# The carry copies moved out of the Exp pair in a prefix log-sum-exp scan on one core

## Chip, cores, metric

One core of one Trainium2 chip. The metric is the device time of one execution in microseconds. Executions fall into states. "Slow" means over 1.5% above the fastest execution of the same kernel; means and ratios below use fast executions only.

## The reference

```python
B, S, D = (8, 4096, 2048)                      # float32
out[:, 0, :] = x[:, 0, :]
for t in range(1, S):                          # running log-sum-exp along S
    mx = np.maximum(out[:, t-1, :], x[:, t, :])
    out[:, t, :] = mx + np.log(np.exp(out[:, t-1, :] - mx) + np.exp(x[:, t, :] - mx))
```

The kernel computes it as log(cumulative sum(exp(x))). It works on 64 tiles of 128 partitions x 4 rows x 2048 columns (4 MB each): load, Exp, sums of four rows and across partitions, Ln, store.

## The kernel before

Six tile buffers `ti` stand in a ring. SyncE issues the loads, each when the store of the same buffer has landed. ScalarE does the Exp, a small copy and the Ln, in two halves of the columns, and issues the stores. The copy carries the last 32 partitions of the finished tile n-1 into `rs`, from which the sums of tile n are begun. It waits for DVE's last addition of tile n-1 (`joined`), and DVE's third addition of tile n waits for it (`copied`).

```python
            @block.sync
            def _(sp):
                ...
                        take(sp, stored[n], 16)                       # the buffer's store has landed
                        load(x_v[bass.ds(j * NI + n, 1)][0], n)
            @block.scalar
            def _(act):
                def exp(n, h, rows=slice(0, R)):
                    ...  # for h == 0: waits for the load; Exp in place; exps[h] += 1
                def copy(n, h, turn):
                    act.activation(
                        rs[P - 32:, half(h)], ti[n % NI][P - 32:, R - 1, half(h)], ACT.Copy
                    )._wait_ge(joined[h], turn + 1).then_inc(moved, 1)
                    event(act, [(moved, 2 * turn + h + 1)], [(copied[h], "sem-add-imm", 1)])
                ...
                with act.Fori(0, turns) as j:
                    for n in range(1, NI + 1):
                        for h in range(2):
                            exp(n, h)
                            copy(n - 1, h, n - 1)
                        for h in range(2):
                            ln(n - 1, h)
                        store(n - 1, o_v[bass.ds(j * NI + (n - 1), 1)][0], 2 * n)
                    settle(NI, NI, 2 * NI)
                ...
            @block.vector
            def _(dve):
                def local(n, h):
                    ...  # two additions, the first after exps[h]
                    dve.wait_ge(copied[h], n + 1)
                    dve.tensor_add(
                        rs[:P - 1, cols], t[:P - 1, 2, cols], t[:P - 1, 3, cols]
                    )._wait_ge(chain[h], 3 * n + 2).then_inc(sums[h], 1)
```

The softmax here doesn't subtract the row's maximum and nothing guards it: scores larger than these inputs give would overflow.

Of the kernel before, what the change touches and what calls it, by code (L numbers as in the profile page):

```python
# [9 lines left out]
def kernel(  # L10
# [30 lines left out]
    NT = B * NBLK  # L41
# [16 lines left out]
    def half(h):  # L58
        return slice(h * HALF, (h + 1) * HALF)

    def event(engine, waits, updates):

        engine.add_instruction(mybir.InstEventSemaphore(  # L63
            name=f"I-{nc.next_id()}", engine=engine.engine, ins=[], outs=[],
            sync_info=mybir.SyncInfo(
                on_wait=[mybir.SyncWait(
                    sync_type="semaphore", id=s.num, ant_name=s.name,
                    wait_mode="sem-ge-imm", wait_value=n,
                ) for s, n in waits],
                on_update=[mybir.SyncUpdate(  # L70
                    sync_type="semaphore", id=s.num, ant_name=s.name,
                    update_mode=mode, update_value=n,
                ) for s, mode, n in updates],
            ),
        ))

    def take(engine, s, n):

        event(engine, [(s, n)], [(s, "sem-sub-imm", n)])

    with tc.tile_critical():  # L81
# [12 lines left out]
        with nc.Block() as block:  # L94

            @block.gpsimd
            def _(g):
                g.memset(before[:], 1.0).then_inc(ones, 1)  # L98
                g.wait_ge(ones, 1)

                g.affine_select(  # L101
                    out=before[:], in_=before[:], compare_op=mybir.AluOpType.is_ge, fill=0.0,
                    base=-1, pattern=[[1, P]], channel_multiplier=-1,
                ).then_inc(shaped, 1)
                g.wait_ge(shaped, 1)

                g.affine_select(  # L107
                    out=before[:], in_=before[:], compare_op=mybir.AluOpType.is_ge, fill=1.0,
                    base=P - 2, pattern=[[0, P]], channel_multiplier=-1,
                ).then_inc(shaped, 1)  # L110

                for h in range(2):
                    g.sem_inc(copied[h], 1)
# [22 lines left out]
# [3 lines that stand above are left out]
                    t = ti[n % NI]  # L139
                    if h == 0:  # L140
                        take(act, loaded[n % NI], 16)
                    act.activation(  # L142
                        t[:, rows, half(h)], t[:, rows, half(h)], ACT.Exp
                    ).then_inc(exps[h], 1)
# [8 lines that stand above are left out]
                def ln(n, h, rows=slice(0, R)):  # L153
                    t = ti[n % NI]
                    act.activation(  # L155
                        t[:, rows, half(h)], t[:, rows, half(h)], ACT.Ln
                    ).then_inc(logs, 1)

                def store(n, dst, done, rows=slice(0, R)):
                    act.wait_ge(logs, done)  # L160
                    act.dma_start(  # L161
                        out=dst[:, rows, :], in_=ti[n % NI][:, rows, :]
                    ).then_inc(stored[n % NI], 16)

                def settle(turns, copies, done):
                    take(act, moved, 2 * copies)
                    take(act, joined[0], turns)
                    take(act, joined[1], turns)
                    take(act, logs, done)

                take(act, top, 16)
                act.activation(ti[0][:, 0:2, :], ti[0][:, 0:2, :], ACT.Exp)  # L172
                exp(0, 0, slice(2, R))
                exp(0, 1, slice(2, R))
                turns = (NT - 2) // NI
                with act.Fori(0, turns) as j:
                    for n in range(1, NI + 1):
                        for h in range(2):
                            exp(n, h)
                            copy(n - 1, h, n - 1)  # L180
                        for h in range(2):
                            ln(n - 1, h)
                        store(n - 1, o_v[bass.ds(j * NI + (n - 1), 1)][0], 2 * n)
                    settle(NI, NI, 2 * NI)
                first = turns * NI
                for n in range(first + 1, NT):

                    early = n == NT - 1
                    for h in range(2):
                        if not early:  # L190
                            exp(n, h)
                        copy(n - 1, h, n - 1 - first)
                        if early and h == 0:
                            ln(n - 1, h)
                        if early:
                            exp(n, h)
                    for h in range(early, 2):
                        ln(n - 1, h)
                    store(n - 1, o_v[n - 1], 2 * (n - first))

                turn = NT - 1 - first
                act.wait_ge(joined[0], turn + 1)
                ln(NT - 1, 0)
                act.wait_ge(joined[1], turn + 1)
                done = 2 * turn + 1
                for rows in LAST:
                    ln(NT - 1, 1, rows)
                    done += 1
                    store(NT - 1, o_v[NT - 1], done, rows)
                settle(NT - first, NT - 1 - first, done)  # L210
# [91 lines left out]
```

## Time and profile before

| | the kernel before |
|---|---|
| three timed executions | 1252.88, 1254.04, 1254.31 us |
| profiled execution | 1279.36 us, slow |
| DMA queues, share of 16 engines | loads 49.6%, stores 49.1% |
| busy: ScalarE, DVE, TensorE | 82%, 82%, 32% |
| load, store: issue to landing (median) | 36.8 us, 45.4 us |

The prediction shows how the profile of before is read. From the timeline of the kernel before (start, us, engine, line, operation; in brackets the idle time before it and what ended that):

```profile
23.14 3.62 ACT L142 ACTIVATE ti<-ti 128x4096 f32<-128x4096 f32 x1 [6.00 <-ACTq L63]
...
27.38 1.05 ACT L148 ACTIVATE rs<-ti 32x1024 f32<-32x1024 f32 x1 [0.62 <-DVE ti L253]
...
40.67 0.40 ACTq L161 DMA_DIRECT2D out_dram<-ti  x1
```

Exp of tile 1 runs as soon as its load is there, and the first store of the run is issued at 40.67 us.

### The profile page before, as it was taken

The numbers are of one execution on the slowest core, as the hardware profiler recorded it, in microseconds if no ns is written. First come the engines' busy times: TensorE is split into PE (matmuls) and PEld (weight loads), VectorE is DVE, ScalarE is ACT, GpSimd is POOL, SyncE is SP. The second block draws the span as 40 slices with busy tenths as digits, with TensorE's granted clock in tenths as the row PEclk, the third lists the DMA queues.
The fourth block names the chain that finished last, engine by engine and source line by source line (L and its number), as shares of the span: only waits on it lengthen the run. The fifth ranks groups of instructions, "written<-read, shape, count | busy, mean of one in ns | idle before, by whom it ended". The sixth has DMA issues, their size and how long they took to land. (4 is left out here: it accounts for less than half of the span.)

```text
span 1277.6 us, 3085 instructions
## 1 busy us (share of the span) xinstructions
PE 409.4 (32%) x512; PEld 131.9 (10%) x512; DVE 1044.3 (82%) x640; ACT 1053.0 (82%) x385; POOL 1.0 (0%) x7
## 2 busy tenths in 40 slices
PE   1334342324223242232422324233242341432412
PEld 0111110101001010010100101011010010110100
DVE  5999998878788787887878788787887888878874
ACT  5999998877878778787887878788788787888883
POOL 0000000000000000000000000000000000000000
PEclk9766567655666656766567666566666666656665
DMA  9999999999999999999999999999999999999976
GB/s 398 423 431 432 428 433 429 428 432 428 431 427 429 426 432 428 425 427 425 426 423 427 431 425 422 433 429 426 429 428 420 428 425 426 422 426 429 424 323 282
DMA packets 18727, 536.96 MB, mean 420 GB/s; under 512 B 2081, under 2 KB 2081, under 8 KB 2081
## 3 DMA queue, kind: packets, MB, share of 16 engines
q1 hardware_dynamic: 9360, 268.44, 49.6%
q10 hardware_dynamic: 9360, 268.44, 49.1%
q8 instruction: 4, 0.07, 0.0%
q14 instruction: 3, 0.02, 0.0%
HBM read 268.44 MB, written 268.44 MB: 420 GB/s over the span
## 5 line engine op out<-in xcount | busy, mean ns | idle before, releaser
L218 PE MATMUL ps<-rs,before 128*128 128x512 f32 (+1 forms) x512 | 409.4, 946 | 845.3 <-DVE rs L243 845.2
L142 ACT ACTIVATE ti<-ti 128x4096 f32<-128x4096 f32 (+1 forms) x128 | 459.4, 3590 | 186.1 <-ACTq L63 178.3
L155 ACT ACTIVATE ti<-ti 128x4096 f32<-128x4096 f32 x129 | 456.3, 3582 | 13.9 <-DVE ti L253 5.7
L249 DVE TENSOR_TENSOR ti<-ti,ps 128x3072 f32<-128x3072 f32 x128 | 428.4, 3347 | 1.1 <-PE ps L218 1.1
L236 DVE TENSOR_TENSOR ti<-ti 128x1024 f32<-128x1024 f32 x128 | 156.8, 1225 | 201.4 <-ACT ti L142 201.4
L218 PEld LDWEIGHTS ps<-rs,before 128*128 128x128 f32 (+1 forms) x512 | 131.9, 285 | 1121.4 <-DVE rs L243 1009.8
L253 DVE TENSOR_TENSOR ti<-ti 128x1024 f32<-128x1024 f32 x128 | 156.8, 1225 | 4.4
L243 DVE TENSOR_TENSOR rs<-ti 127x1024 f32<-127x1024 f32 x128 | 156.8, 1225 | 4.4
L239 DVE TENSOR_TENSOR ti<-ti 128x1024 f32<-128x1024 f32 x128 | 156.8, 1225 | 4.4
L148 ACT ACTIVATE rs<-ti 32x1024 f32<-32x1024 f32 x126 | 132.6, 1052 | 4.1 <-DVE ti L253 0.6
L172 ACT ACTIVATE ti<-ti 128x4096 f32<-128x4096 f32 x1 | 3.6, 3616 | 6.5 <-ACTq L63 6.5
L35 ACT ACT_TABLE_LOAD x1 | 1.3, 1283 | 0.8 <-PEq L286 0.8
L107 POOL TENSOR_SCALAR_AFFINE_SELECT before<-before 128x128 f32<-128x128 f32 x1 | 0.3, 292 | 0.1
L101 POOL TENSOR_SCALAR_AFFINE_SELECT before<-before 128x128 f32<-128x128 f32 x1 | 0.3, 292 | 0.1
L98 POOL MEMSET before<- 128x128 f32 x1 | 0.2, 204 | 0.5 <-SPq L81 0.5
L286 POOL MEMSET const-bfloat16-1.0<- 128x1 bf16 x1 | 0.1, 101 | 0.0
L286 POOL MEMSET const-uint8-127<- 128x1 uint8 x1 | 0.1, 101 | 0.0
L286 POOL MEMSET const-float32-0.0<- 128x1 f32 x1 | 0.1, 98 | 0.3 <-issue 0.3
L286 POOL MEMSET const-float32-1.0<- 128x1 f32 x1 | 0.1, 98 | 0.0
## 6 DMA issues: line engine op xcount, KB each, us to landing
ti<-in_x_dram SPq DMA_DIRECT2D x63, 4096.0 KB, 36.8
out_dram<-ti ACTq DMA_DIRECT2D x63, 4096.0 KB, 45.4
ti<-in_x_dram SPq DMA_DIRECT2D x2, 2048.0 KB, 9.6
out_dram<-ti ACTq DMA_DIRECT2D x2, 2048.0 KB, 10.6
```

Of the source, the lines that this page charges most:

```text
L35: nc.scalar.preload_act_table_set("natural_log_exp_and_others")
L142: act.activation(t[:, rows, half(h)], t[:, rows, half(h)], ACT.Exp).then_inc(exps[h], 1)
L148: act.activation(rs[P - 32:, half(h)], ti[n % NI][P - 32:, R - 1, half(h)], ACT.Copy)._wait_ge(joined[h], turn + 1).then_inc(moved, 1)
L155: act.activation(t[:, rows, half(h)], t[:, rows, half(h)], ACT.Ln).then_inc(logs, 1)
L172: act.activation(ti[0][:, 0:2, :], ti[0][:, 0:2, :], ACT.Exp)
L218: m = pe.matmul(ps[n % 2][:, sl], before[:k, :], rs[:k, sl], start=True, stop=True,)
L236: dve.tensor_add(t[:, 1, cols], t[:, 0, cols], t[:, 1, cols])._wait_ge(exps[h], n + 1).then_inc(chain[h], 1)
L239: dve.tensor_add(t[:, 2, cols], t[:, 1, cols], t[:, 2, cols])._wait_ge(chain[h], 3 * n + 1).then_inc(chain[h], 1)
L243: dve.tensor_add(rs[:P - 1, cols], t[:P - 1, 2, cols], t[:P - 1, 3, cols])._wait_ge(chain[h], 3 * n + 2).then_inc(sums[h], 1)
L249: dve.tensor_add(t[:, 0:3, cols], t[:, 0:3, cols], ps[n % 2][:, cols].unsqueeze(1).to_broadcast([P, 3, HALF]),)._wait_ge(ahead[h], n + 1). ...
L253: dve.tensor_add(t[:, 3, cols], t[:, 2, cols], t[:, 3, cols])._wait_ge(chain[h], 3 * n + 3).then_inc(joined[h], 1)
L286: nc = _bacc.Bacc("TRN2", target_bir_lowering=False, num_devices=1)
```

## The change

It is meant to fill ScalarE's wait for the load with the first copy, and to put the second one behind both Exp halves, so that the Exp pair runs without a gap.

```diff
+                def step(n, turn, early=False):
+                    copy(n - 1, 0, turn)
+                    if early:
+                        ln(n - 1, 0)
+                    exp(n, 0)
+                    exp(n, 1)
+                    copy(n - 1, 1, turn)
+                    if not early:
+                        ln(n - 1, 0)
+                    ln(n - 1, 1)
@@ in the loop
-                        for h in range(2):
-                            exp(n, h)
-                            copy(n - 1, h, n - 1)
-                        for h in range(2):
-                            ln(n - 1, h)
+                        step(n, n - 1)
@@ in the last steps (early: n is the last tile)
-                    (Exp, copy, Exp, copy, Ln, Ln; for the last tile copy, Ln, Exp, copy, Exp, Ln)
+                    step(n, n - 1 - first, n == NT - 1)
```

(The line in parentheses stands for eleven lines of the same kind, which are cut here.)

More of the change, by code (lines that the diff above doesn't have):

```diff
@@ L186, in _ @@
                 for n in range(first + 1, NT):
-                    early = n == NT - 1
-                    for h in range(2):
-                        if not early:
-                            exp(n, h)
-                        copy(n - 1, h, n - 1 - first)
-                        if early and h == 0:
-                            ln(n - 1, h)
-                        if early:
-                            exp(n, h)
-                    for h in range(early, 2):
-                        ln(n - 1, h)
+                    step(n, n - 1 - first, n == NT - 1)
                     store(n - 1, o_v[n - 1], 2 * (n - first))
```

## The prediction

> **What bounds the kernel now.** I read the page first, then the wait table, then stretches of time, one tile period of the timeline, and last the DMA record of the final 48 us. The profiled execution took 1279.36 us and is marked slow, against 1254.04 us for the timed runs. I take its order of events and its instruction times over to the fast runs, but not its length.
>
> From the page's DMA queues (packets, MB, share of 16 engines' span) and from the wait table (us in total, times, longest us):
>
> ```profile
> q1 hardware_dynamic: 9360, 268.44, 49.6%
> q10 hardware_dynamic: 9360, 268.44, 49.1%
> DVE ti L236 <- ACT ti L142: 201.4, 113, 15.4
> ACT ti L142 <- ACTq L63: 178.3, 63, 6.0
> ```
>
> The queue of the loads and the queue of the stores together hold the 16 DMA engines for 98.7% of the span. ScalarE waits 178.3 us in 63 waits ahead of an Exp, about 2.8 us a tile, for the load. That looks like time to be won, but the stretches say what stands behind it (columns: stretch and length, busy us of each engine, clock, DMA share, GB/s):
>
> ```profile
> 100.00:400.00 300.00, 103.54 (x128) 33.29 (x128) 258.77 (x159) 257.48 (x95) 0.00 (x0) 0.63 1.00 430
> 400.00:800.00 400.00, 128.45 (x160) 40.99 (x160) 324.74 (x200) 328.70 (x120) 0.00 (x0) 0.63 1.00 426
> 800.00:1180.00 380.00, 121.88 (x152) 39.11 (x152) 312.83 (x192) 315.04 (x115) 0.00 (x0) 0.64 1.00 427
> ```
>
> The DMA share is 1.00 throughout, while DVE (324.74 of 400) and ScalarE (328.70 of 400) are at 81 and 82%. A load is issued 36.8 us before it lands (median on the page) and a tile period is 20 us (400 us for 160/8 = 20 tiles), so the next load is always already queued when one lands. ScalarE waits for DMA bandwidth, not for somebody to start a load.
>
> One period in the timeline (start, us, engine, line, operation; idle before it in brackets), ScalarE's Exp, copy, Exp, copy, Ln pair, and the DVE result that the first copy needs:
>
> ```profile
> 615.28 1.23 DVE L253 TENSOR_TENSOR ti<-ti 128x1024 f32<-128x1024 f32 x1
> 616.69 0.34 ACTq L161 DMA_DIRECT2D out_dram<-ti  x1
> 619.96 3.62 ACT L142 ACTIVATE ti<-ti 128x4096 f32<-128x4096 f32 x1 [3.44 <-ACTq L63]
> 623.61 1.05 ACT L148 ACTIVATE rs<-ti 32x1024 f32<-32x1024 f32 x1
> 624.78 3.62 ACT L142 ACTIVATE ti<-ti 128x4096 f32<-128x4096 f32 x1
> 628.42 1.05 ACT L148 ACTIVATE rs<-ti 32x1024 f32<-32x1024 f32 x1
> 629.60 7.12 ACT L155 ACTIVATE ti<-ti 128x4096 f32<-128x4096 f32 x2
> ```
>
> The value for the first copy is ready at 616.51; ScalarE is free at 617.03 (after issuing the store) and then waits until 619.96. A copy of 1.05 us fits.
>
> The end decides whether shortening a chain shows. GB/s of the last 48.5 us in 40 slices of 1.213 us:
>
> ```profile
> GB/s 81 81 81 81 432 432 432 432 432 432 432 432 81 81 81 81 81 81 432 432 432 432 432 432 432 432 54 189 419 392 378 378 432 432 432 432 54 41 14 0
> ```
>
> Full speed is 432, so one engine is 27 and 81 is three engines working while thirteen stand idle. The two blocks of eight slices are the stores of tiles 61 and 62. Between them 13 engines pause, but three never do: they lag. The trace's completion events say the same: the sixteen engines complete the second load within 0.5 us of each other, the last load only within 20 us, and a store around 1150 us within 30 us. Tile 62's store was issued at 1250.77, yet its last engine finished only at 1266.5, while tile 63's first half-store was issued at 1262.03. The slowest engine therefore had 4.5 us of queued work when the final store was issued: it is busy from the first load to the last byte, and sets the end. The page's short chain of ScalarE and DVE work at the end runs beside it.
>
> **What the Trainium skill says.** "DMA: Bandwidth & Descriptors", section "Specifications", gives a fabric ceiling of 435 GB/s over 16 engines; the 426 to 430 GB/s above agree, so there is no bandwidth left to win. The same page, "Queues, rings and completion order", says that each DMA engine serves its queue rows round robin by packets. The trace agrees: from 60 to 80 us the load queue holds 50.5% and the store queue 49.0%, whereas from 20 to 40 us, before the first store, loads hold 99.0%. Its section "Why a DMA increments its semaphore by 16 and not by 1" says that only the full 16 means that all has landed, which is why the slowest engine paces everybody. "ScalarE: Activation LUTs", section "What ACT_TABLE_LOAD costs", gives 186 ns + 0.833 ns per element, with back-to-back instructions overlapping by about 93 ns: 3598 ns for 4096 elements (trace 3617) and 1039 for 1024 (trace 1052); the two Ln, 7.12 us instead of 7.23, show the overlap. The page shows a single table load, so a new order of Exp, Copy and Ln costs none.
>
> **The change part by part.** No instruction and no byte is added or removed: 128 Exp-type, 126 copy and 129 Ln instructions stay. Only ScalarE's order changes.
>
> 1. First copy into the load wait. Before, the second Exp started 624.78 - 619.96 = 4.82 us after the first; after, 3.62 less the overlap, about 3.55. That takes about 1.2 us from Exp pair to store, so the store issue comes 1.2 us sooner after the load lands. On the path in steady state: 0. The store only waits longer in a queue that always holds work (45.4 us from issue to landing), and the next load starts when that store has landed.
> 2. Second copy behind both Exps. DVE's second local chain started 4.81 us after the first (1242.45 to 1247.26 at the end); now it starts after the three adds, about 3.67. DVE's third add needs that copy 2.4 us into its chain, and the copy ends about 1.1 us into it, so no new wait. Gain 1.1 us of latency, also 0 while DMA is full.
> 3. Start. copy(0,0) now stands before exp(1,0) and needs DVE's join of tile 0, which ends at 27.35, whereas exp(1,0) ran at 23.14. ScalarE stalls and the first store moves from 40.67 to 27.38 + 1.15 + 3.6 + 3.55 + 1.15 + 7.1 = 44 us, some 3.4 us later. Until then the loads have the engines alone at full rate, so the engines lose nothing. From then on both queues are full and share equally, so loads stay ahead by 3.4 us. The load queue shrinks from 36.8 to about 30 us, still more than a period.
> 4. Tail. From exp(62,0) at 1216.93, released by a load, ScalarE runs nearly without idle time to the end. Two copies (2 x 1.17 with their gaps) leave this chain, so the last half-stores are issued 2.3 us sooner, up to 5.7 with the head start of step 3. But the slowest engine had 4.5 us of work queued at that point, so this becomes a longer queue.
>
> Sum: 0 in steady state, 0 at the start, 0 in the tail. A check by bytes: an engine moves 128 transfers x 8 packets of 32 KB at a median of 1.213 us (trace), 1242 us, and the first packets run from about 3.4 us, so 1245.5 is an estimated floor of the span. The measured time exceeded the span by 1.8 us in the profiled run; so the fast span is about 1252.3, only 6.8 us above the floor, for packets over the median and the last completion. A fast-run tail with sixteen even engines, by the same steps, lands load 63 near 1207, issues the first half of store 63 near 1232 and has the engines busy with store 62 until 1236: hidden too, by some 3 us.
>
> **Rivals.**
> (a) Filling the wait pays on each tile. 63 tiles x 1.2 us = 76 us, so 1178 us. For it: 178.3 us of waits. Against it: DMA share 1.00 and the floor of 1245.5 + 1.8 = 1247.
> (b) In fast runs the lag is small and the tail chain is exposed: -2.3 us, or -5.7 with the head start, 1248.3 to 1251.7. For it: thirteen engines do pause in the tail. Against it: the margin worked out above, in both states. I give it a sixth.
> (c) The stall at the start reaches the end, +3.4 us, 1257.4; or loads that land early make the copy stand in the way of Exp. For it: up to about 190 us ScalarE hardly waits (0.64 us a tile, period 17.4). Against it: the DMA share is already 1.00 there and the loads run ahead.
>
> **Range and chances.** The centre is the time before, less a little for (b): 1253.8. The three runs spread by 1.4 us and another chip or session may shift by some 0.2%; with (b) and (c) that gives 1250.5 to 1257. Two per cent is 25 us: faster is excluded by the floor, slower only by an engine state that the kernel doesn't choose.
>
> **What would show it.** Second Exp about 3.55 us after the first, the first copy inside the load wait, ScalarE's idle time still near 3 us a tile (same work, same period; only its place moves), first store near 44 us, load issue to landing shorter by some 7 us and stores longer by as much, DMA share 1.00 up to the tail, and at least one engine never idle. I am wrong if the DMA share falls below 1.00 in mid-run, if all sixteen engines pause before the last store, or if the time moves by over 4 us in runs of the same state.

## The result, and the profile after

The changed kernel took 1250.70 us (median of 4, 1250.40 to 1250.88), the kernel before beside it 1254.17 us (median of 4, 1252.88 to 1254.69). The ratio is 0.9974, 95% interval 0.9956 to 0.9991. Such a ratio is the mean time of one kernel's fast runs over that of the other's of the same rounds, so it is not quite the ratio of the medians. The predicted range was 1250.5 to 1257 us; its centre of 1253.8 was 3.1 us too high.

The profiled execution after was fast (span 1249.0 us), that of before slow. Where lengths are compared, I therefore use a second profile of the kernel before, from run E1 below, which is fast (span 1253.2 us).

The order is as intended. From the timeline after, one period:

```profile
615.10 1.22 DVE L250 TENSOR_TENSOR ti<-ti 128x1024 f32<-128x1024 f32 x1
616.06 0.34 ACTq L173 DMA_DIRECT2D out_dram<-ti  x1
616.45 1.05 ACT L148 ACTIVATE rs<-ti 32x1024 f32<-32x1024 f32 x1 [0.55 <-DVE ti L250]
619.63 1.22 DVE L250 TENSOR_TENSOR ti<-ti 128x1024 f32<-128x1024 f32 x1
619.88 7.12 ACT L142 ACTIVATE ti<-ti 128x4096 f32<-128x4096 f32 x2 [2.38 <-ACTq L63]
627.02 1.05 ACT L148 ACTIVATE rs<-ti 32x1024 f32<-32x1024 f32 x1
628.20 7.12 ACT L155 ACTIVATE ti<-ti 128x4096 f32<-128x4096 f32 x2
```

The copy stands in the load wait and both Exp halves take 7.12 us together. From Exp start to store issue it is now 15.6 us (619.88 to 635.49, the next store) against some 16.9 before (619.96 to 636.88). But ScalarE still waits 2.38 us for the load, and the period is 619.88 - 600.45 = 19.43 us. The wait tables tell the same, first the kernel before, then the changed one (us in total, times, longest us):

```profile
DVE ti L236 <- ACT ti L142: 176.9, 112, 15.4
ACT ti L142 <- ACTq L63: 153.7, 63, 6.0
```

```profile
DVE ti L233 <- ACT ti L142: 155.9, 64, 15.2
ACT ti L142 <- ACTq L63: 109.2, 63, 2.4
ACT rs L148 <- DVE ti L250: 39.1, 53, 10.5
ACT rs L148 <- ACTq L63: 12.3, 10, 1.3
```

Of the 153.7 us of load waits 44.5 are gone, and 51.4 us of waits ahead of the copies have come (10.5 of them once, at the start). The waits were moved, not shortened. The stretches show why (stretch and length, busy us of PE, PEld, DVE, ScalarE and POOL, granted clock, DMA share, GB/s):

```profile
100.00:400.00 300.00, 102.02 (x136) 35.03 (x136) 270.88 (x168) 272.75 (x101) 0.00 (x0) 0.65 1.00 433
400.00:800.00 400.00, 120.41 (x161) 41.08 (x160) 335.12 (x206) 335.71 (x124) 0.00 (x0) 0.64 1.00 433
800.00:1180.00 380.00, 123.29 (x160) 41.88 (x160) 320.67 (x198) 320.91 (x119) 0.00 (x0) 0.64 1.00 433
```

The DMA share is 1.00 as before. What did change is the start, the queues and the end. Timeline of the start, after:

```profile
27.49 1.05 ACT L148 ACTIVATE rs<-ti 32x1024 f32<-32x1024 f32 x1 [10.49 <-DVE ti L250]
28.75 7.13 ACT L142 ACTIVATE ti<-ti 128x4096 f32<-128x4096 f32 x2 [0.21 <-ACTq L63]
...
44.38 0.40 ACTq L173 DMA_DIRECT2D out_dram<-ti  x1
```

The first copy waits 10.49 us for DVE and holds up the first Exp pair; the first store is issued 3.4 us later than in E1 (40.95 us) and 3.7 us later than in the slow profile (40.67 us). Meanwhile loads run alone. The DMA queues between 40 and 60 us (packets, MB, share), before in the fast state, then after:

```profile
q1 hardware_dynamic: 175, 4.72, 58.3%
q10 hardware_dynamic: 112, 3.67, 42.5%
```

```profile
q1 hardware_dynamic: 207, 5.73, 70.1%
q10 hardware_dynamic: 81, 2.65, 30.7%
```

The loads (q1) got 1 MB more in this stretch. Counted from the packets of the trace, loads are ahead of stores by 4.1 to 4.3 tiles through the whole fast run before, and by 4.5 to 4.7 through the whole run after: the lead of the first 48 us is kept for 1200. The page's list of DMA issues (KB each, median us from issue to landing), before, then after:

```profile
ti<-in_x_dram SPq DMA_DIRECT2D x63, 4096.0 KB, 36.2
out_dram<-ti ACTq DMA_DIRECT2D x63, 4096.0 KB, 43.9
```

```profile
ti<-in_x_dram SPq DMA_DIRECT2D x63, 4096.0 KB, 26.5
out_dram<-ti ACTq DMA_DIRECT2D x63, 4096.0 KB, 54.6
```

A load stands in its queue 9.7 us less and a store 10.7 us more. The last view is GB/s of the last 48.5 us in slices of 1.213 us, the time of one 32 KB packet, so 432 is all sixteen engines and 27 is one. Before, then after:

```profile
GB/s 432 432 432 432 432 432 432 432 432 432 432 432 432 432 432 162 54 54 432 432 432 432 432 432 432 432 27 230 432 432 405 419 432 419 392 311 27 27 14 0
```

```profile
GB/s 432 432 432 432 432 432 432 432 432 432 432 432 432 432 459 432 432 432 432 432 432 459 459 432 432 432 365 405 432 432 432 432 432 432 365 135 27 27 0 0
```

Before, ten to fourteen engines pause for three slices while the others catch up, and fifteen in one later slice (the 27); after, hardly any pauses before the last slices. In the trace's completion events, the sixteen engines end the last load within 10.0 us of each other before and within 4.2 us after. So the 3.4 us should be time of one or two slow engines. Whether the new order, the later first store or chance did that, the two profiles can't say.

### The profile page after: what moved, and what is told of

Read it like the earlier page. It is cut to its first block, busy times and chain, and to the rows that moved or that the text cites. A ratio compares the mean times of both kernels' runs of the same rounds, so it can differ in the third digit from the quotient of the medians.

```text
span 1249.0 us, 3085 instructions
## 1 busy us (share of the span) xinstructions
PE 385.3 (31%) x512; PEld 131.3 (11%) x512; DVE 1044.3 (84%) x640; ACT 1046.2 (84%) x385; POOL 1.0 (0%) x7
## 5 line engine op out<-in xcount | busy, mean ns | idle before, releaser
L215 PE MATMUL ps<-rs,before 128*128 128x512 f32 (+1 forms) x512 | 385.3, 905 | 831.7 <-DVE rs L240 831.0
L142 ACT ACTIVATE ti<-ti 128x4096 f32<-128x4096 f32 (+1 forms) x128 | 452.5, 3582 | 109.2 <-ACTq L63 109.2
```

What stands on the lines that cost most here:

```text
L142: act.activation(t[:, rows, half(h)], t[:, rows, half(h)], ACT.Exp).then_inc(exps[h], 1)
L215: m = pe.matmul(ps[n % 2][:, sl], before[:k, :], rs[:k, sl], start=True, stop=True,)
```

## The experiments

Twelve runs were made, all correct, each on one chip together with the kernel before. Theory D: the slowest DMA engine has work queued from the first load to the end, so chains on ScalarE are worth nothing, and what was won is engine time. Rival T: the chain at the end is exposed, and the two copies taken from it are the gain. To these came theory S, that the later first store is the cause, and L, luck.

The kernel before turned out not to have one time. Its 49 executions go from 1249.61 to 1300.96 us: 15 lie below 1251.2, 3 up to 1253, 24 between 1253 and 1260, and 7 above. For such a spread, the share of executions up to 1253 us says more than a mean.

**E1, the kernel before again.** No edit.

> The kernel before, unchanged, against itself: gives the noise, and, it is hoped, a profile of it in the fast state. Ratio 1.000 within 0.002 by every theory. Theory D (slowest DMA engine decides, and the 3.4 us won are engine time lost in packets longer than 1.213 us in the old order): the fast profile shows DMA share 1.00 to the end, the final half-stores issued several us before store 62 has landed, and a larger sum of over-long packets than the 2 us per engine of the changed kernel. Theory T (tail chain exposed): the fast profile shows all sixteen engines pausing for 2 to 4 us between store 62 and store 63, or before store 62.

1254.95, 1254.64, 1249.70, 1249.63, 1249.71 and 1282.31 us; ratio of the fast ones to those of the reference runs 0.9977 (0.9953 to 1.0002). So a kernel differs from itself by as much as the change had won. The fast profile (its tail is shown above) has all engines busy to the end but for pauses of those that wait for the slowest two; tile 63's first half-store is issued at 1237.61, and store 62's last engine completes at 1242.1, 4.5 us later. That speaks for D. And three executions at 1249.6 to 1249.7, below the best of the changed kernel, show that the old order's chain does not cost 2 to 4 us as such.

**E2, the new order in the first step only** (first turn of the loop unrolled):

```diff
-                    step(n, n - 1)                     # all steps
+                    (step if n == 1 else step_old)(n, n - 1)
```

> New order in the first step only (the first copy waits for DVE, first store near 44 us instead of 40.7), the old order in all others; the first turn of the loop is unrolled. If the head start of the loads is what pays: about 1250.8 us, -3.4. If the shorter chain per tile or in the tail pays: 1254.2 +- 0.7. If the stall at the start costs: up to +3.4.

1251.36 us median, all six between 1250.12 and 1251.80; ratio 0.9978 (0.9959 to 0.9996). The ratio alone would prove nothing beside E1's 0.9977, but no execution lies in the group above 1253 us, with 62 of 63 steps in the old order. The timeline shows the late start:

```profile
27.34 1.05 ACT L148 ACTIVATE rs<-ti 32x1024 f32<-32x1024 f32 x1 [10.21 <-DVE ti L267]
...
44.08 0.39 ACTq L185 DMA_DIRECT2D out_dram<-ti  x1
```

**E3, the new order in all steps but the first**, and **G3, the same kernel again**:

```diff
-                    step(n, n - 1)
+                    (step_old if n == 1 else step)(n, n - 1)
```

> New order everywhere but in the first step, so the first store stays at 40.7 us. If the head start pays: 1254.2, no gain. If the shorter chain pays: 1250.8 to 1251.9.

> E3 again, on another chip perhaps: new order in all steps but the first. If the order of the later steps matters beside the head start: most executions at 1250 to 1251. If only the head start matters: a spread as in the kernel before of the same call, with executions above 1253.

The first store of E3 is back in its old place:

```profile
40.76 0.39 ACTq L185 DMA_DIRECT2D out_dram<-ti  x1
```

E3: 1250.89, 1253.61, 1256.39, 1253.40, 1250.99, 1251.04; ratio 0.9995 (0.9973 to 1.0017). G3: 1250.82, 1253.19, 1250.72, 1258.31, 1250.84, 1251.08; ratio 0.9997 (0.9969 to 1.0025). Without the late first store the times fall into the two groups again, at 1251 and at 1253 to 1258. 7 of these 12 lie at or below 1253, against 10 of 34 of the kernel before, so a small share of the later steps in the effect is not excluded. They don't suffice for it. The first turn of the loop is unrolled here as in E2, so the unrolling is not what keeps E2's times together.

The two runs also show a cost. Their seven good executions (1250.72 to 1251.08, mean 1250.91) all lie above the fifteen good ones of the kernel before (1249.61 to 1250.09, mean 1249.76). So where the engines keep in step, the new order of the later steps costs about 1.1 us. In the profile of E3 the slowest engine ends the last load at 1206.4 us and the others by 1203.7; in that of G4 below (old order) it is 1205.3 and 1203.5. Why one engine ends later is not shown.

**E4, the new order in the last two steps only**, where it takes two copies from the chain to the last store:

> New order in the last two steps only (62 and 63); the two copies leave the chain to the last store, 2.3 us sooner. Theory T (tail chain exposed): -2.3 us, 1251.9. Theory D or head start: 1254.2 +- 0.7, as the engines still have work queued.

Median 1255.72 us (1249.96 to 1263.55), ratio 1.0006 (0.9982 to 1.0029). No gain. T expected 2.3 us less. The chain did become shorter: from the start of Exp of tile 62 to the issue of the first last half-store it took 42.97 us, against 45.09 in E1.

**F1, the changed kernel again**, and **F2, F3: the old order in all steps, with small copies that are waited for ahead of the first store**, five or ten of 1.16 us:

```diff
+                    if n == 1:
+                        act.wait_ge(logs, 2)
+                        for _ in range(5):             # F3: 10, G2: 2
+                            act.activation(spare[:], ti[0][:, 0, 0:1024], ACT.Copy).then_inc(paused, 1)
+                            take(act, paused, 1)
                     store(n - 1, o_v[n - 1], 2 * n)
```

> The changed kernel again, for its spread on the same chip as the runs beside it. Theory S (the head start shifts the two streams against each other, and that avoids most of the over-long packets): six executions all between 1250 and 1252, while the kernel before has most at 1253.5 to 1255 and a few near 1250. Theory L (luck: both kernels draw from the same spread): executions of both spread over 1250 to 1257.

> The old order throughout, with five small waited-for copies (about 5.8 us together) ahead of the first store, so first store data starts near 50.2 us instead of 44.4, loads ahead of stores by about 4.8 tiles instead of 4.2. Theory S: 1250 to 1252 in all executions, under 50 packets over 1.3 us, although no copy has been moved. If the moved copies themselves matter: as before, 1254.5. If a later first store costs its delay: +5.8, 1260.

> As f2 with ten copies, 11.6 us: first store data near 56 us, loads ahead by about 5.4 tiles. If what matters is the lead in whole tiles (lead 4.2 and 5.2 alike bad, 4.6 good): somewhat bad again, median 1252 to 1255. If any larger lead is good: 1250 to 1252. If a later first store costs: +11.6, 1266.

F1: 1250.66 us, all six within 1250.24 to 1250.78. F2: 1251.18 us, 1250.62 to 1251.66. F3: 1252.17 us, 1251.61 to 1252.86. The kernel before beside them: seven of eleven at 1249.61 to 1252.89, two at 1254.16 and 1255.90, two slow at 1284.94 and 1300.96. On this chip its good executions were frequent, so the ratios of the fast runs are 0.9993, 0.9998 and 1.0005: no gain in the mean. The narrow times of F2 and F3 agree with S: the late first store alone, without a moved copy, seems to make them so. On this chip that is weak evidence, as seven of the nine fast executions of the kernel before were good too; G2 below repeats the test on a chip where five of fourteen were. My number for F3's lead was wrong. It should have been 5.4 tiles; the trace shows 4.5 to 4.8, as in F2. The ring of six buffers explains it: in F3 the last queued load landed at 68.39 us, and the next could be issued only at 72.53, when the first store had landed, so for 4 us no load was queued. So F3 did not test whether whole tiles matter. The delay costs 0.5 us (F2) and 1.5 us (F3) over F1, and 1.4 and 2.4 us over the good executions of the kernel before (1249.8 in the mean), not 5.8 and 11.6 us.

**G2, the same with two copies**, 2.3 us:

> The old order with two waited-for copies (about 2.3 us) ahead of the first store: first store data near 46.7 us. If any delay of that size gives the lead: all six executions between 1249.8 and 1251.5. If the lead must come near its limit of some 4.6 to 4.7 tiles: mixed, some executions above 1253, as in the kernel before.

1250.34 us median, 1249.97 to 1250.84; ratio 0.9978 (0.9957 to 0.9999). Loads lead by 4.4 to 4.6 tiles. A delay of this size is enough:

```profile
40.80 2.24 ACT L207 ACTIVATE spare<-ti 128x1024 f32<-128x1024 f32 x2
43.15 0.38 ACTq L187 DMA_DIRECT2D out_dram<-ti  x1
```

It is the lowest median of the kernels whose six executions all stay together, but F1 ran on another chip, so it is not shown to beat the changed kernel.

**F4, the changed kernel with eight waited-for copies ahead of its last two half-stores:**

```diff
                 act.wait_ge(joined[1], turn + 1)
+                for _ in range(8):
+                    act.activation(spare[:], rs[:, 0:1024], ACT.Copy).then_inc(paused, 1)
+                    take(act, paused, 1)
```

> The changed kernel with eight waited-for copies (about 9.3 us) in the chain ahead of the last two half-stores. Theory D (the engines have some 11 us of stores queued there): no change, 1250.7 +- 0.6. If the chain at the end decided: +9.3, 1260. This tells what the 2.3 us taken from that chain can have been worth.

1250.92 us (1250.70 to 1250.98), 0.26 us over F1 on the same chip. The timeline of F4 shows that the delay was real:

```profile
1224.33 9.30 ACT L205 ACTIVATE spare<-rs 128x1024 f32<-128x1024 f32 x8 [0.91 <-DVE ti L255]
...
1235.70 0.34 ACTq L175 DMA_DIRECT2D out_dram<-ti  x1
```

In the changed kernel that issue was at 1225.95. GB/s of the last 48.5 us of F4, again in slices of one packet:

```profile
GB/s 459 432 432 432 432 432 432 432 432 432 432 432 432 432 432 432 432 432 432 432 432 432 432 432 432 432 270 108 27 230 432 432 432 432 432 432 432 230 0 0
```

Most engines now pause before the last two half-stores, but one is still at work (the 27), and the end hardly moves. 9.3 us more in the chain cost 0.26 us. So the 2.3 us that the change took from it can't have been worth more than some tenths of a microsecond there.

**G4, the kernel before with three such copies in its tail**, 3.5 us:

> The kernel before with three waited-for copies (about 3.5 us) in the chain ahead of its last two half-stores. Theory D (4 to 5 us of stores queued on the slowest engine there): fast executions as those of the kernel before, within 0.7 us like for like (best near 1249.7). If the tail chain decided: every execution 3.5 us longer, best at 1253.1.

1249.74, 1249.92, 1249.80, 1249.82, 1256.33, 1256.48; ratio 0.9994 (0.9965 to 1.0024). Four executions lie at the kernel's best, 0.1 to 0.3 us above 1249.63. T wanted 1253.1 or more in all. T is out for the old order too. The delay in its timeline:

```profile
1229.08 3.41 ACT L208 ACTIVATE spare<-rs 128x1024 f32<-128x1024 f32 x3 [0.91 <-DVE ti L258]
```

**G1, the kernel before a third time:**

> The kernel before once more, in the hope of a profile at its best time (1249.6). Theory D says that such an execution has under 50 packets over 1.3 us, no slowest engine far behind (completions of a store spread by under 5 us at the end), and no idle time of all engines in the tail. Theory T would have the tail pause in it. If the profile falls at 1254 to 1257 instead, it should show one or a few engines that never pause and 60 to 300 long packets.

1254.88, 1283.76, 1280.76, 1249.65, 1253.68, 1249.97; ratio 0.9983 (0.9952 to 1.0014). Its profile fell on 1254.88. So no profile of the unedited kernel at its best exists; the profile of G4 at 1249.74 stands in for it, the old order with the first store issued in its old place (40.89).

What separates the executions can be counted in the traces: 32 KB packets that took 1.313 us or more (at least 0.1 us over the median of 1.213), in the first 100 us and later.

| profile | us of that execution | first store data, us | over-long, to 100 us | later |
|---|---|---|---|---|
| before (slow) | 1279.36 | 44.3 | 44 | 566 |
| E4 | 1263.55 | 44.4 | 33 | 228 |
| E1 (before) | 1254.95 | 44.4 | 20 | 47 |
| G1 (before) | 1254.88 | 44.3 | 26 | 88 |
| E3, G3 | 1250.89, 1250.82 | 44.4, 44.5 | 32, 24 | 5, 7 |
| G4 | 1249.74 | 45.9 | 19 | 4 |
| after, F1, F4 | 1250.72, 1250.78, 1250.93 | 48.2, 49.6, 48.3 | 29, 29, 31 | 5, 5, 5 |
| E2, G2 | 1251.80, 1249.97 | 48.4, 47.1 | 26, 24 | 5, 6 |
| F2 | 1251.24 | 50.9 | 29 | 6 |
| F3 | 1252.86 | 56.6 | 67 | 6 |

Every execution at 1253 us or more that was profiled has many over-long packets in the steady part; every one below has four to seven. Of the 16,128 packets that is little. But added up over all engines, the later ones took 6.8 us more than the median in E1 and 11.5 us in G1, against 1.6 to 2.4 us in the good executions. The spans of E1 and G1 are 5.2 and 5.1 us longer than that of G4, and in the last load one engine of E1 and two of G1 end over 5 us behind the rest. So nearly all of the excess must fall on these one or two engines, and the slowest sets the end. The old order can do without over-long packets too (G4), so it isn't bound to have them; it is only open to them. With the first store delayed (after, F1, F4, E2, F2, F3, G2) 40 of 40 executions are at or below 1252.86. With it at its old place, the kernel before has 18 of 49 at or below 1253 (18 of 42 without the slow ones), and E3, G3, E4 and G4 together 12 of 24.

**Open.** Why the late first store keeps the engines in step is not settled. The larger lead of the loads and the shorter load queue (24.1 to 29.8 us from issue to landing instead of 33.7 to 36.4) come with it in every run, and no run separates the two. In G1, 78 of the 88 later over-long packets begin within 3 us after a store's issue, and in E1 42 of 47, where chance would give some 15% (3 us of a period of 19.4); in E4 it is 58 of 228 and in the slow profile 179 of 566. That may be a hint, but no run tests it. In G4 the first store's data began 1.5 us later than in the other undelayed runs although it was issued as early, yet the lead stayed at 4.1 to 4.3 tiles; whether that matters is open too. The trace doesn't name the engine of a packet.

## Why the prediction was right, and where it was not

1. *First copy into the load wait, 0 in steady state.* Right: 44.5 us of load waits became 51.4 us of waits ahead of the copies at DMA share 1.00, and E3 and G3, which have it without the late start, gain nothing that their spread lets one see. It is not quite 0, however: their good executions are about 1.1 us longer than those of the kernel before, which the prediction did not foresee. I had said about 1.2 us sooner from Exp to store; the two timelines show 1.3.
2. *Second copy, 0 while DMA is full.* Right by the same runs. One correction: in the usual step the second copy already stood behind both Exp halves. It moves only in the step of the last tile, so items 1 and 2 of the prediction count one and the same gain in the steady part.
3. *Start: first store 3.4 us later, the engines lose nothing.* The stall is right (predicted near 44 us, measured 44.38; no DMA time lost). Queue times went the right way but further than said: 9.7 us less for loads and 10.7 us more for stores instead of about 7. This is the step that failed in its worth: I put 0 on it, and E2 and G2, beside E3 and G3, show that it is what makes the difference.
4. *Tail: up to 5.7 us sooner, hidden.* Right: E4 without a gain, F4 with 9.3 us more for 0.26 us, G4 with 3.5 us more for 0.1 to 0.3.

The sum was 0; the first comparison gave -3.4 us. The mis-sized term is the one of the check by bytes, "only 6.8 us above the floor, for packets over the median and the last completion". I treated it as a property of the chip that both kernels share. It is not: by the same sum it is 2.5 us in G4 (span 1248.0) and 3.5 us after (span 1249.0), and the change decides how often an execution is good. One reading in that sum was wrong: the first packets start at 2.04 to 2.41 us, not at 3.4, so the floor is nearer 1244.4 and each of these rests 1 us more; what they say of each other stays. (A count was off too: the page lists 129 Exp instructions, 128 on L142 and one on L172.) Rival (b) named the measured size (1248.3 to 1251.7), but for an exposed tail chain, which F4 and G4 exclude. As predicted, the engines never all pause: in no profile is there a moment between the first load and the last byte when all sixteen are idle. My condition "if the time moves by over 4 us" was not met.

The size of the gain depends on how often the kernel before is in step: 3.4 us in the medians of the first comparison, 2.0 us in those beside F1 with its two slow executions counted; without these its median there is 1249.84, 0.8 us below F1's. Its best (1249.61) is 0.6 us below the changed kernel's best (1250.24). What the change brings surely is the narrow spread, 1250.24 to 1250.88 in all ten executions.

## What to carry to other kernels

When two full DMA queues share the engines all through a kernel, shortening the engines' chains need not gain anything. Look also at how the queues start: the moment of the first store set the lead of the loads for the whole run here. A filled wait was worth nothing here, as what it waits for is bandwidth (E3, G3); lengthening a chain on purpose, as F4 does at the end, shows in one run what shortening it could be worth. And run the unchanged kernel against itself before explaining a fraction of a per cent.

## What the Trainium skill lacked or had wrong

- "DMA: Bandwidth & Descriptors", section "Latency and other measured facts", offers for two DMA engines that are usually slower a best guess, the rings of the software queue, and calls that specific to it. It has nothing for the case here: only the two hardware queues carry the data, and one to four engines still fall behind. The sixteen engines' completions of the last load are spread over 20 us in the slow run, 10 us in E1 and 2.3 to 4.6 us in the good ones. The trace doesn't name the engines, so whether they are the two of the page is not shown.
- No page says that the DMA packets of one kernel can differ between executions: 47, 88 or 566 packets of 1.313 us or more after the first 100 us in three profiles of the kernel before, and 1249.61 to 1300.96 us for its executions.
- "DMA: Bandwidth & Descriptors", section "Queues, rings and completion order", states the round robin between queue rows. The equal shares here (50.2% and 50.1% from 100 to 1180 us) agree, but don't test it, as each load also waits for a store. No page says how long the lead lasts that one queue has when the second becomes full: here it stayed at 4.2 or 4.6 tiles over 1200 us, and whether the round robin or the ring of buffers keeps it is not shown.
